# Five and six sevens in the first feed-forward's second product, with x loaded behind them

## The chip, the cores and the metric

The kernel runs on one core of one Trainium2 chip. The metric is the device time of one execution in microseconds; of several runs the median counts. Engines are named as in the profile: PE (TensorE: matmuls and transposes), DVE (VectorE), ACT (ScalarE), POOL (GpSimd, here almost only the issue of DMAs) and SP (SyncE, which issues the loads of weights).

## What is computed

One layer of a Conformer-like block over 256 tokens of width 2048, all in float32. Only the two feed-forwards are touched by the change; a mixer (convolution and gated spatial mixing) and a cross-attention with four heads stand between them.

```python
def swiglu_ffn(h, w_in, w_out):          # w_in 2048 x 11264, w_out 5632 x 2048
    gate, up = jnp.split(h @ w_in, 2, axis=-1)
    return (jax.nn.silu(gate) * up) @ w_out

x = x + 0.5 * swiglu_ffn(rms(x), ffn1_w_in, ffn1_w_out)
# ... mixer, cross-attention ...
x = x + 0.5 * swiglu_ffn(rms(x), ffn2_w_in, ffn2_w_out)
# final rms
```

## The kernel before

**A float32 product in three matmuls.** Every operand is kept as two parts of a reduced format, hi and lo, and a product is hi x hi + hi x lo + lo x hi. A weight tile ("raw", 128 x 1024, 512 KB) is loaded by SP; ACT casts it to hi (L396), DVE subtracts hi from raw to get lo (L397), both into a tile "hl". The transposed input (x_hl, or hA, hB, hC for the hidden values) has been split in the same way.

**Eights and sevens.** The k of a product are taken in pairs, two blocks of 128 rows of the weight. An "eight" multiplies a pair plainly: 24 matmuls of 512 columns, 12 for each of two weights. A "seven" takes the pair as a 2 x 2 block product with seven products instead of eight: 21 matmuls. Its weights are sums: DVE makes them with four half-width operations (L464, L465, L471, L478), and three and a half weights are cast and subtracted. Its left sides are sums too, prepared once (`out_sides`: one copy and two casts by ACT, four small sums and two subtracts by DVE for each pair that is ever a seven) and kept in `out_forms`. A weight of an eight feeds 12 matmuls in a row; of a seven's first weights PE uses two matmuls, then the next weight is wanted.

**The first feed-forward's second product** runs in two blocks of 1024 output columns (`out_block`, NG + 0 and NG + 1), each over 22 pairs in the order OUT_STEPS; OUT_S names the pairs that are sevens. In block 0 the transposes of the last hidden values ("turns", which write hB and hC, L131 and L132) run beside the first eights, so the sevens come behind them. In block 1 the sevens come first, with two eights between one and the next; the transposes of block 0's output o and the joins into x (`joins`, a DVE operation into xT, then x_hl and squares) run beside the eights that follow. When a block's last seven is done, its sums are copied to o and added there (ACT L515, DVE L516 to L519).

**Buffers.** Weights rotate through three tiles hl and a ring; in these blocks the ring has two tiles of more_out, whose other half holds four forms. Raw tiles rotate through four of a pool and those in `ff.raws`: for block 0 four raws_out, which lie in the place of xT (x is not needed there), and two raw_out; between the blocks xT is taken back and loaded again by two DMAs of POOL's queue (2 MB, L773), and block 1 has the pool and raw_out. When block 1's last seven is issued, the ring is emptied.

**Summed weights.** For some k (SUMMED) the lo part is not subtracted by DVE: ACT writes -raw and hi (L425, L426, in `summed`), and a DMA of POOL's queue adds the weight a second time from memory onto it (L427). The tile is hl_s; in the second feed-forward (`pair`) there is a second one up to group 7, and from group 8 on only one. The first two are issued in `run`: `summed(0)` in group 0 behind k = 13, `summed(1)` behind group 0.

**Order.** Instructions are placed on each engine by a scheduler that simulates the program with costs of its own, within the order of the code, the buffers and `tc.issue_after`. Each engine then runs its own list strictly in order: an instruction that waits holds all behind it.

## Time and profile before

| | us |
|---|---|
| runs | 2098.36, 2094.91, 2098.84; median 2098.36 |
| profiled execution | 2097.01 |
| its span in the trace | 2095.2 |
| PE busy | 2080.0 (99%) |
| DVE busy | 1621.0 (77%) |
| ACT busy | 1175.0 (56%) |

Busy shares are averages over stages; what counts for the time is where PE stands still. In a timeline the first number is the start and the second the length in us; matmuls are pipelined and their lengths overlap, so pace is read from start to start. In brackets stands how long the engine was idle before, and what it waited for.

### The profile page before, as it was taken

The page shows a single profiled execution, that of the slowest core. Times are in us where ns is not written, and L with a number is a line of the kernel's source. Part 1 is how long each engine was busy: PE and PEld are TensorE (multiplying, and loading weights), DVE is VectorE, ACT ScalarE, POOL GpSimd, SP SyncE. Part 2 cuts the span into 40 slices and gives each one's busy share as a digit, 9 for nine tenths or more (in the row PEclk, how much of TensorE's full clock was granted, in tenths as well). Part 3 has the DMA queues.
Part 4 walks back from the last instruction along what each step waited for, and adds up shares of the span by engine and source line. Part 5 has one row for each costly group of instructions (what it writes and reads, how often), then busy time and mean ns, then how long its engine had stood idle before and what let it go on. Part 6 is the DMA issues. An engine that isn't in the chain of part 4 may idle for free.

```text
span 2095.2 us, 26732 instructions
## 1 busy us (share of the span) xinstructions
PE 2080.0 (99%) x9765; PEld 1738.5 (83%) x9765; DVE 1621.0 (77%) x2300; ACT 1175.0 (56%) x1472; POOL 67.7 (3%) x83
## 2 busy tenths in 40 slices
PE   9999999999999999999999999999999999999998
PEld 8888888888788888888888898888888888888886
DVE  7888887877777679989877666778888878787754
ACT  8665666555546554445664455556665656554443
POOL 0000000000000000000000000000000000000000
PEclk9999999999999999999999999999999999999999
DMA  9787778755457566555555544677777777556664
GB/s 366 242 260 249 227 226 263 229 182 202 169 201 233 181 237 203 183 180 185 181 195 191 186 157 130 215 269 221 233 242 245 225 221 235 176 163 203 195 193 152
DMA packets 122532, 442.35 MB, mean 211 GB/s; under 512 B 13600, under 2 KB 13984, under 8 KB 122016
## 3 DMA queue, kind: packets, MB, share of 16 engines
q1 hardware_dynamic: 113184, 407.08, 56.4%
q0 software_dynamic: 8640, 32.51, 8.3%
q8 instruction: 76, 1.25, 0.2%
q10 hardware_dynamic: 576, 1.06, 0.1%
q14 instruction: 56, 0.46, 0.1%
HBM read 438.49 MB, written 2.10 MB: 210 GB/s over the span
## 4 chain that ended last, share of the span: by engine, by line
PE 81%; issue 15%; DMA 2%; POOL 1%; ACT 1%; DVE 1%; SPq 0%; DVEq 0%; POOLq 0%; ACTq 0%
PE acc L331 9%; PE acc L333 9%; PE acc L330 9%; PE acc L204 8%; PE acc L203 8%; PE acc L202 8%; PE acc L153 8%; PE acc L161 4%; PE acc L318 2%; PE acc L319 2%; PE acc L317 2%; PE aux L305 1%; POOL hl_s L427 1%; PE acc L1278 1%; PE acc L1277 1%
## 5 line engine op out<-in xcount | busy, mean ns | idle before, releaser
L123 ACT CAST hl<-raw 128x1024 fp32r<-128x1024 f32 (+1 forms) x315 | 327.1, 1040 | 356.1 <-PE acc L204 194.7
L124 DVE TENSOR_TENSOR hl<-raw,hl 128x1024 fp32r<-128x1024 f32 (+1 forms) x315 | 381.2, 1212 | 166.8 <-ACT hl L123 165.4
L397 DVE TENSOR_TENSOR hl<-raw,hl 128x1024 fp32r<-128x1024 f32 (+1 forms) x144 | 164.6, 1145 | 51.2 <-ACT hl L396 49.9
L396 ACT CAST hl<-raw 128x1024 fp32r<-128x1024 f32 (+1 forms) x144 | 141.0, 988 | 110.2 <-PE acc L333 51.4
L397 DVE TENSOR_TENSOR hl<-spare,hl 128x1024 fp32r<-128x1024 f32 (+1 forms) x128 | 146.9, 1152 | 37.3 <-ACT hl L396 34.6
L396 ACT CAST hl<-spare 128x1024 fp32r<-128x1024 f32 (+1 forms) x128 | 126.2, 993 | 73.3 <-PE acc L333 25.4
L331 PE MATMUL acc<-hl,x_hl 128*128 128x512 f32 x408 | 148.2, 391 | 0.1
L330 PE MATMUL acc<-hl,x_hl 128*128 128x512 f32 x408 | 142.4, 391 | 0.0
L333 PE MATMUL acc<-hl,x_hl 128*128 128x512 f32 x408 | 126.6, 389 | 0.0
L396 ACT CAST ring<-spare 128x1024 fp32r<-128x1024 f32 (+1 forms) x81 | 80.5, 998 | 59.3 <-issue 20.4
L397 DVE TENSOR_TENSOR ring<-spare,ring 128x1024 fp32r<-128x1024 f32 (+1 forms) x81 | 93.3, 1157 | 14.8 <-ACT ring L396 13.6
L203 PE MATMUL acc<-hl,x_hl 128*128 128x512 f32 x256 | 100.6, 393 | 0.0
L203 PE MATMUL acc<-hl,m_hl 128*128 128x512 f32 x256 | 100.3, 392 | 0.0
L204 PE MATMUL acc<-hl,m_hl 128*128 128x512 f32 x256 | 100.2, 392 | 0.0
L204 PE MATMUL acc<-hl,x_hl 128*128 128x512 f32 x256 | 99.9, 390 | 0.0
L331 PE MATMUL acc<-ring,x_hl 128*128 128x512 f32 x248 | 91.4, 389 | 0.0
L202 PE MATMUL acc<-hl,m_hl 128*128 128x512 f32 x256 | 90.9, 392 | 0.0
L202 PE MATMUL acc<-hl,x_hl 128*128 128x512 f32 x256 | 90.2, 392 | 0.0
L330 PEld LDWEIGHTS acc<-hl,x_hl 128*128 128x128 f32 x408 | 76.6, 188 | 16.2 <-ACT hl L396 0.4
L333 PEld LDWEIGHTS acc<-hl,x_hl 128*128 128x128 f32 x408 | 76.7, 188 | 16.0
L331 PEld LDWEIGHTS acc<-hl,x_hl 128*128 128x128 f32 x408 | 76.3, 188 | 16.4 <-DVE hl L397 0.8
L330 PE MATMUL acc<-ring,x_hl 128*128 128x512 f32 x248 | 88.8, 389 | 0.0
(515 smaller groups left out, 5115.2 us busy)
## 6 DMA issues: line engine op xcount, KB each, us to landing
spare<-in_ffn_w_in SPq DMA_DIRECT2D x185, 512.0 KB, 6.8
raw<-in_ffn_w_in SPq DMA_DIRECT2D x156, 512.0 KB, 6.3
raw<-in_ffn_w_out SPq DMA_DIRECT2D x135, 512.0 KB, 4.0
hl_s<-in_ffn_w_in POOLq DMA_DIRECT2D x44, 512.0 KB, 8.7
raw<-in_w_mix_vg SPq DMA_DIRECT2D x32, 512.0 KB, 4.5
raw<-in_w_k SPq DMA_DIRECT2D x32, 512.0 KB, 3.6
raw<-in_w_v SPq DMA_DIRECT2D x32, 512.0 KB, 4.3
raw<-in_w_mix_out SPq DMA_DIRECT2D x32, 512.0 KB, 4.6
```

The costliest lines, as they stand in the source:

```text
L123: nc.scalar.copy(out=hl[:, 0, :size], in_=raw[:, :size])
L124: newest[0] = nc.vector.tensor_tensor(out=hl[:, 1, :size], in0=raw[:, :size], in1=hl[:, 0, :size].bitcast(F32), op=ALU.subtract)
L153: done = nc.tensor.matmul(acc, lhsT=hi[:, k], rhs=xs[k], start=first and k == 0, stop=last and k == kk - 1, skip_group_check=True,)
L161: done = nc.tensor.matmul(acc[:, 0], lhsT=lo[:, k], rhs=xs[k][:, 0], start=False, stop=last and k == kk - 1, skip_group_check=True,)
L202: nc.tensor.matmul(acc[t], lhsT=x[:, 0, s], rhs=hi[:, k], start=k0 + k == 0, stop=False)
L203: nc.tensor.matmul(acc[t], lhsT=x[:, 0, s], rhs=lo[:, k], start=False, stop=False)
L204: nc.tensor.matmul(acc[t], lhsT=x[:, 1, s], rhs=hi[:, k], start=False, stop=k0 + k == nk - 1)
L330: nc.tensor.matmul(acc[t][g], lhsT=x[:, 0, s], rhs=hi[:, cols[g]], start=(t, g) in first, stop=False)
L331: nc.tensor.matmul(acc[t][g], lhsT=x[:, 0, s], rhs=lo[:, cols[g]], start=False, stop=False)
L333: nc.tensor.matmul(acc[t][g], lhsT=x[:, 1, s], rhs=hi[:, cols[g]], start=False, stop=last)
L396: self.cast = nc.scalar.copy(out=hl[:, 0, :n], in_=raw[:, :n])
L397: newest[0] = nc.vector.tensor_tensor(out=hl[:, 1, :n], in0=raw[:, :n], in1=hl[:, 0, :n].bitcast(F32), op=ALU.subtract)
```

## The change

Five things are changed. Sevens: three become five in block 0 and four become six in block 1, each followed by one eight while they last. Buffers: six forms instead of four, so the ring has one tile of more_out and a tile of its own, hl_out, which stays when the sevens end; the two raw_out are gone, and raws_out serve both blocks. x: its two loads are issued when block 1's last seven is, and the turns of block 0's output are handed out from step 14 on instead of step 10. Summed weights: the second feed-forward's groups 8 to 10 have k = 2 and 10 instead of 2, 7 and 13. `summed_then`: the first two summed weights are issued only behind the newest load and the newest cast. Line numbers of the kernel after are one higher around L396 (L397, L398), and more further down.

```diff
@@ -37,13 +37,14 @@
 PATTERNS = ("SCSCSCCC", "SCSCSCCC")
 
 SUMMED = ((2, 7, 13), (2, 7, 13))
-
-
-
-OUT_S = ((9, 12, 15), (9, 12, 15, 18))
+ALONE = (2, 10)
+
+
+
+OUT_S = ((9, 11, 13, 15, 17), (9, 11, 13, 15, 17, 19))
 OUT_STEPS = (
-    [0, 1, 2, 3, 4, 5, 6, 7, 8, 10, 11, 9, 13, 14, 12, 16, 17, 15, 18, 19, 20, 21],
-    [9, 0, 1, 12, 2, 3, 15, 4, 5, 18, 6, 7, 8, 10, 11, 13, 14, 16, 17, 19, 20, 21],
+    [0, 1, 2, 3, 4, 5, 6, 7, 8, 10, 9, 12, 11, 14, 13, 16, 15, 18, 17, 19, 20, 21],
+    [9, 0, 11, 1, 13, 2, 15, 3, 17, 4, 19, 5, 6, 7, 8, 10, 12, 14, 16, 18, 20, 21],
 )
 
 
@@ -404,7 +405,7 @@
             self.raw_at += 1
             raw = wraw.tile([P, 1024], F32, name="raw") if i < 4 else self.raws[i - 4]
 
-            nc.sync.dma_start(out=raw, in_=self.w_in[j, :, k] if j < NG else self.w_out[j - NG, :, k])
+            self.load = nc.sync.dma_start(out=raw, in_=self.w_in[j, :, k] if j < NG else self.w_out[j - NG, :, k])
             return raw
 
         def buffer(self, at):
@@ -425,6 +426,11 @@
             nc.scalar.activation(out=hl[:, 1], in_=raw, func=AF.Copy, scale=-1.0)
             nc.scalar.copy(out=hl[:, 0], in_=raw)
             nc.gpsimd.dma_start(out=hl[:, 1], in_=self.w_in[j, :, k], accum_op=ALU.add)
+
+        def summed_then(self, at):
+
+            with tc.issue_after(self.load.ins), tc.issue_after(self.cast.ins):
+                self.summed(at)
 
         def sides(self, i):
 
@@ -605,6 +611,9 @@
             acc = token_accs()
             sums = self.pattern_sums
             self.sums_at = [(j, k) for j in range(1, NG) for k in sums if j < NG - 1 or k < min(14, sums[-1])]
+            if self.pair:
+
+                self.sums_at = [at for at in self.sums_at if at[0] < 8] + [(j, k) for j in range(8, NG) for k in ALONE]
             for k in range(KD):
                 if k == 0 and early:
                     w = self.early(before)
@@ -617,12 +626,12 @@
                 if k == 13:
                     r = root()
                     nc.scalar.activation(out=st.tile([P, 1], F32, name="warm"), in_=ones[:, 0:1], func=AF.Silu)
-                    self.summed(0)
+                    self.summed_then(0)
             self.give(0, [acc[t][0] for t in range(2)], [acc[t][1] for t in range(2)], r)
             if more is not None:
                 more()
             if len(self.hls) > 1:
-                self.summed(1)
+                self.summed_then(1)
             turns = [self.turn(i) for i in range(2 * NG)]
             for j in range(1, NG):
                 if j < NG - 1:
@@ -747,10 +756,10 @@
         def turns_first(i):
             if i == 0:
                 more = big.tile([P, 4, 2, 1024], F32R, name="more_out", tag="S2")
-                ff.ring += [more[:, q] for q in range(2)]
-                forms = more[:, 2:].rearrange("p a two n -> p (a two n)")
+                ff.ring.append(more[:, 0])
+                forms = more[:, 1:].rearrange("p a two n -> p (a two n)")
                 ff.out_forms = [
-                    forms[:, q * 1024:(q + 1) * 1024].rearrange("p (f two n) -> p f two n", two=2, n=P) for q in range(4)
+                    forms[:, q * 1024:(q + 1) * 1024].rearrange("p (f two n) -> p f two n", two=2, n=P) for q in range(6)
                 ]
             next_turn()
             if i == 8:
@@ -758,7 +767,7 @@
                 ff.high.close()
                 pool = rest["pool"] = stack.enter_context(tc.tile_pool(name="ffn1", bufs=1, reuse_waits="tile"))
                 ff.sums = pool.tile([P, 1024], F32, name="sums_out")
-                ff.raws += [pool.tile([P, 1024], F32, name=f"raw_out{q}") for q in range(2)]
+                ff.ring.append(pool.tile([P, 2, 1024], F32R, name="hl_out"))
 
         def result():
             return rest["pool"].tile([P, 2, 2 * G], F32, name="o", bufs=2)
@@ -767,19 +776,20 @@
             return [turning(o, 2 * i * P, joins(8 * n + 2 * i)) for i in range(4)]
 
         o = ff.out_block(0, result, turns_first, next_turn)
-        ff.raws = ff.raws[4:]
-        xT = xt.tile([P, KD, T], F32, name="xT", tag="x")
-        for k in range(0, KD, 8):
-            nc.gpsimd.dma_start(out=xT[:, k:k + 8], in_=a["xT"][:, k:k + 8])
         turns += turned(o, 0)
 
         def beside_second(i):
+            nonlocal xT
             if i == OUT_STEPS[1].index(OUT_S[1][-1]):
-                ff.ring = []
+
+                ff.raws, ff.ring = [], ff.ring[1:]
+                xT = xt.tile([P, KD, T], F32, name="xT", tag="x")
+                for k in range(0, KD, 8):
+                    nc.gpsimd.dma_start(out=xT[:, k:k + 8], in_=a["xT"][:, k:k + 8])
                 rest["x_hl"] = gained_tile("S2")
-            elif i > 9:
+            elif i > 10:
                 beside(1.4)
-                if i % 2 == 0 and turns:
+                if i > 12 and i % 2 == 0 and turns:
                     turns.pop(0)()
 
         o = ff.out_block(1, result, beside_second)

```

How this moves instructions is shown at three places. First ACT, at the turn into block 0's sevens. Names: hC is the last part of the hidden values, tu and tg are a form's sums, sq is a copy beside them, more_out and hl_out are ring tiles, raw and raw_out are loaded weights, and sums_out are the sums of a seven. Before:

```order
L131 CAST more_out_3525<-tg_3876 128x2x128
L131 CAST hC_3867<-aux_3904 128x2x256
L131 CAST hC_3867<-aux_3927 128x2x256
L131 CAST hC_3867<-aux_3949 128x2x256
L396 CAST more_out_3525<-raw_out0_3961 128x1024
L396 CAST more_out_3525<-sums_out_3960 128x1024
L396 CAST hl_4044<-raw_out1_3962 128x1024
L396 CAST hl_4053<-raw_4031 128x1024
L396 CAST more_out_3525<-raw_4069 128x1024
```

After:

```order
L132 CAST hC_3893<-aux_3918 128x2x256
L132 CAST hC_3893<-aux_3953 128x2x256
L584 COPY sq_3927<-aux_3918 128x256
L132 CAST more_out_3525<-tu_3925 128x2x128
L132 CAST hC_3893<-aux_3976 128x2x256
L397 CAST hl_out_3988<-raw_4026 128x1024
L132 CAST more_out_3525<-tg_3926 128x2x128
L397 CAST hl_4030<-sums_out_3987 128x1024
L397 CAST more_out_3525<-raws_out_3478 128x1024
L397 CAST hl_4057<-raw_4026 128x512
```

Before, the casts of the three last turns stand alone ahead of the first weight (L396), which is an eight's; after, the casts of a form (tu, tg) stand between and behind them, and the first weight is a seven's.

Second PE, behind block 1's last seven. acc are output sums, aux here the transposes of block 0's output o. Before, the first of them come one eight behind that seven (hl_4797 is its second weight):

```order
L331 MATMUL acc_4421<-hl_4797,hA_3455 128x512
L333 MATMUL acc_4420<-hl_4797,hA_3455 128x512
L333 MATMUL acc_4421<-hl_4797,hA_3455 128x512
L305 MATMUL aux_4824<-ident_81,o_4274 128x128 x4
L330 MATMUL acc_4418<-hl_4840,hA_3455 128x512
L331 MATMUL acc_4418<-hl_4840,hA_3455 128x512
```

After:

```order
L320 MATMUL acc_4456<-more_out_3525,hC_3893 128x512
L319 MATMUL acc_4457<-more_out_3525 128x512
L320 MATMUL acc_4457<-more_out_3525 128x512
L306 MATMUL aux_5050<-ident_81,o_4345 128x128 x4
L318 MATMUL acc_4458<-hl_out_3988,hC_3893 128x512
L306 MATMUL aux_5131<-ident_81,o_4345 128x128 x4
L319 MATMUL acc_4458<-hl_out_3988,hC_3893 128x512
L320 MATMUL acc_4458<-hl_out_3988,hC_3893 128x512
L331 MATMUL acc_4456<-hl_out_3988,hA_3455 128x512
```

The transposes of the first two turns have moved into the last seven (L318 to L320 are its matmuls), between matmuls that wait for its last weight.

Third ACT, in the attention's last product (w_o). o_hl is the attention's output, hl_s2 and h8 are the second feed-forward's second summed weight and the tile it is loaded to. Before:

```order
L131 CAST o_hl_9168<-acc_10435 128x256
L123 CAST hl_10508<-raw_10506 128x512
L425 ACTIVATE hl_s2_11172<-h8_11173 128x1024
L426 CAST hl_s2_11172<-h8_11173 128x1024
L123 CAST hl_10528<-raw_10526 128x1024
L123 CAST hl_10557<-raw_10555 128x1024
L280 ACTIVATE x_hl_10466<-xT_4411,pv_82 128x256
```

After:

```order
L132 CAST o_hl_9220<-acc_10487 128x256
L124 CAST hl_10560<-raw_10558 128x512
L124 CAST hl_10580<-raw_10578 128x1024
L124 CAST hl_10609<-raw_10607 128x1024
L281 ACTIVATE x_hl_10518<-xT_4858,pv_82 128x256
L254 ACTIVATE ss_10519<-xT_4858 128x256
```

The two operations on the summed weight are gone from between the casts of w_o's weights; they stand in the second feed-forward's group 0.

## Rows read from the trace of the kernel before

**Rows 1.** The page, part 1: busy us (share of span) xinstructions

```profile
PE 2080.0 (99%) x9765; PEld 1738.5 (83%) x9765; DVE 1621.0 (77%) x2300; ACT 1175.0 (56%) x1472; POOL 67.7 (3%) x83
```

**Rows 2.** Waits of PE, by releaser: us in total, times, longest

```profile
PE acc L331 <- DMA hl_s<-in_ffn_w_in: 1.9, 3, 0.8
```

**Rows 3.** Windows: us, busy (x count) by engine, PEclk, DMA share, GB/s

```profile
540.00:560.00 20.00, 19.45 (x86) 15.74 (x85) 17.92 (x21) 10.85 (x13) 0.00 (x0) 1.00 0.61 205
600.00:620.00 20.00, 20.00 (x90) 16.56 (x89) 17.20 (x20) 10.64 (x12) 0.00 (x0) 1.00 0.72 233
```

**Rows 4.** Timeline of DVE, then ACT, in block 0: start, length, instruction

```profile
552.88 1.22 DVE L397 TENSOR_TENSOR more_out<-raws_out,more_out 128x1024 fp32r<-128x1024 f32 x1
554.02 0.69 DVE L471 TENSOR_TENSOR raw<-sums_out,raw 128x512 f32<-128x512 f32 x1
554.62 0.68 DVE L478 TENSOR_TENSOR raws_out<-raws_out 128x512 f32<-128x512 f32 x1
...
546.80 1.05 ACT L396 CAST hl<-raws_out 128x1024 fp32r<-128x1024 f32 x1
547.75 1.05 ACT L396 CAST hl<-sums_out 128x1024 fp32r<-128x1024 f32 x1
```

**Rows 5.** Timeline of PE, then ACT, before block 0's sevens

```profile
531.99 0.39 PE L330 MATMUL acc<-hl,hB 128*128 128x512 f32 x1
...
533.53 1.20 PE L330 MATMUL acc<-more_out,hB 128*128 128x512 f32 x4 [0.45 <-ACT more_out L396]
...
542.92 0.40 PE L330 MATMUL acc<-more_out,hB 128*128 128x512 f32 x1
531.95 0.59 ACT L131 CAST hC<-aux 128x512 fp32r<-128x512 f32 x1 [3.76 <-PE aux L305]
532.43 1.05 ACT L396 CAST more_out<-raw_out 128x1024 fp32r<-128x1024 f32 x1
```

**Rows 6.** Lines by form, 500 to 530 us: a form's cast

```profile
L131 ACT CAST more_out<-tu 128x256 fp32r<-128x256 f32 x3 | 1.2, 400 | 0.7 <-DVE tu L582 0.7
```

**Rows 7.** Timeline of ACT, then PE, in the w_o product

```profile
1301.87 1.06 ACT L425 ACTIVATE hl_s<-h 128x1024 fp32r<-128x1024 f32 x1 [2.03 <-DMA h<-in_ffn_w_in]
1302.84 1.03 ACT L426 CAST hl_s<-h 128x1024 fp32r<-128x1024 f32 x1
1304.86 1.43 PE L153 MATMUL acc<-o_hl,hl 128*128 128x512 f32 x5 [1.94 <-ACT hl L123]
```

**Rows 8.** Timeline of ACT, then PE, in the first feed-forward's group 0

```profile
32.72 1.04 ACT L425 ACTIVATE hl_s<-spare 128x1024 fp32r<-128x1024 f32 x1
...
35.87 0.61 PE L333 MATMUL acc<-hl,x_hl 128*128 128x512 f32 x2
...
37.76 0.50 PE L331 MATMUL acc<-hl,x_hl 128*128 128x512 f32 x1
```

**Rows 9.** Timeline of PE at two of the three waits for hl_s

```profile
1754.16 0.39 PE L318 MATMUL acc<-hl,x_hl 128*128 128x512 f32 x1
...
1755.52 0.39 PE L330 MATMUL acc<-hl_s,x_hl 128*128 128x512 f32 x1
1756.52 0.72 PE L331 MATMUL acc<-hl_s,x_hl 128*128 128x512 f32 x2 [0.60 <-DMA hl_s<-in_ffn_w_in]
...
1797.92 0.39 PE L330 MATMUL acc<-hl_s,x_hl 128*128 128x512 f32 x1
1799.06 0.73 PE L331 MATMUL acc<-hl_s,x_hl 128*128 128x512 f32 x2 [0.75 <-DMA hl_s<-in_ffn_w_in]
```

**Rows 10.** Transfers into xT, issue to landing

```profile
DMA to landing us min/median/max: 5.2/6.7/8.2
```

**Rows 11.** Windows in the hole of the w_o product and after the last matmul

```profile
1302.00:1305.00 3.00, 1.06 (x7) 0.78 (x7) 1.50 (x5) 3.00 (x4) 0.89 (x1) 1.00 0.45 153
2087.00:2089.00 2.00, 0.00 (x0) 0.00 (x0) 1.06 (x4) 1.54 (x4) 0.67 (x1) 0.99 0.63 260
2089.00:2091.00 2.00, 0.00 (x0) 0.00 (x0) 1.60 (x5) 0.92 (x2) 0.59 (x1) 0.50 0.78 314
```


## The prediction

> **What bounds the kernel now.** I read the page's busy times first: TensorE is busy for 2080.0 of 2095.2 us, VectorE for 77%, ScalarE for 56% [rows 1]. So time is won by taking matmuls away, or by closing one of the few holes in PE; work given to another engine costs only where PE then waits. The waits of PE come second. Of them the change touches one that is listed under one line: three waits for hl_s, 1.9 us in all [rows 2]. Third come the windows around the two out blocks. Where PE is full, VectorE is busy 17.20 of 20 us (86%), and still PE shows no wait; the one window that is not full is the turn into block 0's sevens [rows 3]. So the question is what four more sevens do there, where VectorE has least to give.
>
> The pace is needed for everything that follows. A full subtract takes VectorE 1.14 us from start to start (552.88 to 554.02), a half-width operation 0.60, a full cast takes ScalarE 0.95 (546.80 to 547.75) [rows 4].
>
> **The change part by part.**
>
> *Four eights become sevens.* 24 matmuls become 21, four times: 12 fewer. A matmul of 512 columns starts 0.227 us after the one before it (six of them from 1754.16 to 1755.52) [rows 9]: 12 x 0.227 = -2.7 us, all on the path, since PE is full.
>
> What it adds on VectorE: a seven has three full subtracts, one half-width and four half-width sums, 3 x 1.14 + 5 x 0.60 = 6.4 us, against its 21 x 0.227 = 4.8 us of PE; an eight has two subtracts, 2.3 us against 5.4. Before, a seven stands with two eights: 11.0 us of VectorE for 15.7 of PE, 70%. After, sevens and eights alternate: 8.7 for 10.2, 85%. That is the density of the full window of [rows 3], which runs without a wait, so steady running should cost nothing; what costs is each place where VectorE or ScalarE begins without a lead, because only 1.5 us of lead is made up in 10.2.
>
> *The turn into block 0's sevens.* Before, from 531.99 to 542.92 PE starts 35 matmuls (L330 at 531.99 and those up to 542.92); 35 x 0.227 = 7.9, so 3.0 us of these 10.9 are lost: ScalarE casts the last hC at 531.95, then the first weight at 532.43, and PE has that weight at 533.53 [rows 5]. The first weight feeds an eight, so PE then has 12 matmuls, 2.7 us, in which the next casts run. After, two turns stand together and the first weight's cast stands behind two casts of hC, a copy and one cast of a form instead of behind one cast of hC: 0.59 [rows 5] and 0.40 [rows 6] more, 1.0 us. And it feeds a seven, of which a weight serves two matmuls before the next is wanted: 0.95 of cast against 0.45 of PE, 0.5 us for each of three more weights, 1.5 us. Together +2.5 us; bounds +1.5 (the form's cast hidden) and +4.0 (VectorE's subtracts, 1.14 each, late as well).
>
> *The rest of block 0.* No row shows alternating sevens behind an empty lead. By the 85% it is 0; by one reuse of a ring slot that is cast again as soon as PE lets it go, one cast and half a subtract, some 1.5. I take +1.0.
>
> *Block 1's six sevens.* Below: 0, by the same window. Above: the first seven starts behind block 0's four adds into o (4 x 0.60) with no lead, three weights at 0.5 = 1.5 us; and at the end the four adds of block 1's o, two subtracts of the eights behind it and the adds of the memory's squares stand in VectorE's order ahead of the last half-width subtract of the last seven, for which PE waits: 2.4 + 2.3 + about 1, with the transposes of block 0's o, which were moved to just there and wait for VectorE too: 6 to 7. So 0 to +8. I take +3.0, since the nearest row is the turn into block 0's sevens before, where a lead lost once costs 3.0 [rows 5].
>
> *xT behind the sevens.* Before, it came between the blocks, from POOL's queue. Now the transfer can start only when the last seven's raw tiles are free. Behind it stand, in order, VectorE's join of the first transposes (and then every later subtract) and ScalarE's x_hl operations (and then the next weight's cast), and PE waits for those weights. The two transfers took 5.2 and 8.2 us from issue to landing [rows 10]; the first join needs the first. PE has some 49 matmuls of work that is cast before that wait, 11.1 us, against 5.2 + 0.6 for the join + 1.9 for ScalarE's x_hl (no row shows them there; two casts' time) + 0.95 + 1.14: 9.8. Cost 0, bounds 0 and +3 (if the first lands with the second).
>
> The Trainium skill ("DMA: Bandwidth & Descriptors", section "Anatomy of one DMA — SWDGE (gpsimd) path") gives a transfer from this queue 2.0 us plus its bytes at 436 GB/s: 4.4 us for the first 1 MB, an estimate from that page. The trace's 5.2 is later and decides; by the page the cover would be 0.8 us longer, and the sum the same.
>
> *The w_o product of the attention.* ScalarE waits 2.03 us there for the load of the second feed-forward's summed weight, spends two operations on it from 1301.87, and only then casts the weight for which PE sits idle for 1.94 us [rows 7]. The change issues these operations behind the newest load and cast of the second feed-forward: they leave this place. What is next is the cast itself, whose load was issued before the one that ScalarE waited for. -1.9 us; bound -1 if the second weight there lands late.
>
> *The first feed-forward's start.* The same move takes L425 and L426 (32.72) from ahead of three casts. From 35.87 to 37.76 PE starts six matmuls, 1.36 us of 1.89 [rows 8]: -0.5 us.
>
> *Summed weights of the second feed-forward's last groups.* With one buffer, only 45 matmuls, 10 us, lie between k = 13 of one group and k = 2 of the next, and PE waits for the addition: 1755.52 to 1756.52 and 1797.92 to 1799.06 hold one matmul each, 0.77 + 0.91 us, and the slow pair behind each about 0.1 more [rows 9]: 1.9 us for these two. With k = 2 and 10 there are 78 to 88 matmuls between, 18 to 20 us. The third, into group 8, comes from a group that keeps its 13 and stays. Two summed weights fewer give VectorE two subtracts, which PE does not wait for there. -1.9 us.
>
> **Sum:** -2.7 - 1.9 - 0.5 - 1.9 = -7.0; +2.5 + 1.0 + 3.0 + 0 = +6.5; together -0.5. The profiled execution took 2097.01 us (span 2095.2), so 2096.5; the median of the runs lies 1.35 above that execution, so I say **2097**.
>
> **The rivals.**
>
> *A, the lead holds.* Density of 85% costs nothing, as in [rows 3], in both blocks; only the turn costs: -7.0 + 2.5 = -4.5, 2092.5. For it: 20 us at 86% with a full PE. Against: that window is an average of subtracts for eights, which PE takes 12 matmuls at a time.
>
> *B, VectorE ends last at the end of block 1's sevens.* The adds into o and the joins stand ahead of the subtract for which PE waits; it decides from the point at which VectorE reaches the last seven with less than its 6 us of adds and subtracts in hand. -7.0 + 2.5 + 1.5 + 8 = +5.0, 2102; with xT 3 late as well, 2105: slower, against the median.
>
> *C, the change doesn't do what it says at hl_s.* The waits move to k = 10: -1.9 is lost, 2098.5. Some 18 us from one to the next, where now 10 us lack one, speak against it.
>
> *D, TensorE's clock falls in the longer hole.* It is 1.00 across the hole of w_o, 0.99 in the second after the last matmul and 0.50, 1.2 GHz, from 2089 on, with no matmul in that window or in the one before it [rows 11]. The new hole, some 2.6 us at its longest, lies between. If it fell, the 21 matmuls of the seven behind it would take 4.8 us more: 2101.5. The Trainium skill ("TensorE: Matmul & The Clock Gate", Part 1) says that "the default state is throttled, and activity releases the throttle"; the last row agrees, and no hole inside the kernel shows it.
>
> **How the numbers follow.** Forecast 0.42, A 0.33, B 0.19, C 0.04, D 0.02. A run of this kernel can be told from no change by about 0.2%, 4.2 us around 2098.36. Faster by more is A, 0.33; within it are the forecast, C and D, 0.48; slower by more is B, 0.19, whose lower time lies at the bound. The range runs from A with the turn at its lower bound and a little of the holes' spread (2091) to between B's two times (2104).
>
> **What would show it.** In the profile after: no wait of PE in w_o and none at 36 to 38 us; one wait for hl_s of three; a hole of some 2.5 us at the turn into block 0's sevens, and matmuls missing from the following 20 us against 90 of a full window; in block 1, waits of PE for VectorE at the last seven (rival B if 5 us or more, A if none); ScalarE's first x_hl behind xT not followed by a wait of PE. The forecast is wrong if the two blocks together lose less than 5 us or more than 11 (before: 3.0).

## The result: slower, and where the time went

The kernel after takes 2103.51 us (median of 7 runs, 2102.72 to 2104.46) against 2095.77 of the kernel before (7 runs): a ratio of 1.0032, 95% interval 1.0021 to 1.0044. The forecast was 2097 us, no change that a run could tell. The spans of the two profiled executions differ by 7.5 us (2102.7 and 2095.2).

The page of the kernel after, part 1, in the form of [rows 1]:

```profile
PE 2082.3 (99%) x9753; PEld 1738.2 (83%) x9753; DVE 1639.9 (78%) x2338; ACT 1179.5 (56%) x1484; POOL 66.0 (3%) x81
```

PE has fewer instructions and yet more busy time, in part because some of its matmuls ran at half clock (PEclk in the windows below). PE's waits after (engine line <- released by: us in total, times, longest), where before one line of hl_s stood beside one of w_o; a wait of 1.1 us at the program's start, which both kernels have, is left out:

```profile
PE acc L318 <- ACT hl_out L397: 3.8, 3, 1.8
PE acc L331 <- ACT hl_out L397: 1.4, 1, 1.4
PE acc L319 <- DVE more_out L398: 1.3, 2, 1.1
PE acc L318 <- ACT more_out L397: 1.3, 2, 1.0
PE aux L306 <- DVE o L524: 0.8, 1, 0.8
PE acc L332 <- DMA hl_s<-in_ffn_w_in: 0.4, 1, 0.4
```

The first five of these are all in the out blocks, and two of them name one tile, hl_out. Windows of the kernel after (us, busy of PE, PEld, DVE, ACT and POOL with their counts, PEclk, DMA share, GB/s), to be read beside [rows 3]:

```profile
530.00:536.00 6.00, 4.05 (x11) 2.37 (x11) 6.00 (x11) 4.02 (x6) 0.00 (x0) 0.72 0.01 3
600.00:620.00 20.00, 19.75 (x87) 15.78 (x86) 18.40 (x21) 10.21 (x12) 0.00 (x0) 1.00 0.64 215
652.00:656.00 4.00, 1.92 (x8) 0.98 (x7) 2.94 (x4) 2.87 (x5) 0.00 (x0) 1.00 0.14 37
656.00:660.00 4.00, 1.95 (x9) 1.13 (x8) 3.55 (x7) 1.57 (x2) 0.00 (x0) 1.00 0.93 334
660.00:664.00 4.00, 2.06 (x8) 1.32 (x9) 3.82 (x6) 3.12 (x5) 1.10 (x2) 0.72 0.73 209
664.00:668.00 4.00, 4.00 (x11) 3.14 (x10) 2.65 (x6) 0.59 (x2) 0.00 (x0) 0.50 0.99 408
1300.00:1310.00 10.00, 10.00 (x65) 9.07 (x65) 5.40 (x10) 4.85 (x10) 0.00 (x0) 1.00 0.45 143
```

PE is half empty from 652 to 664, the end of block 1's sevens, and runs at half clock behind that; the hole of w_o ([rows 7]) is closed. The kernel before is full at that place:

```profile
640.00:660.00 20.00, 20.00 (x92) 16.55 (x91) 15.44 (x22) 11.67 (x20) 0.00 (x0) 1.00 0.64 210
```

A sum by place is possible for all of PE's matmuls: the time from one start to the next, less the pace of its kind (0.227 us for 512 columns, 0.120 for 256, 0.109 for a transpose). It is worked out from all rows of both traces:

| place | lost before, us | lost after, us |
|---|---|---|
| first feed-forward, start | 0.65 | 0 |
| turn into block 0's sevens (520 to 550) | 3.0 | 6.15 |
| block 1, start of the sevens (610 to 630) | 0 | 1.85 |
| block 1, last seven (650 to 670) | 0 | 10.1 |
| mixer, at 770 | 0 | 0.65 |
| w_o | 2.2 | 0 |
| hl_s, groups 8 to 10 | 2.75 | 0.65 |
| all other places, about half of it at the program's start | 5.7 | 5.1 |
| all of PE | 14.3 | 24.5 |

24.5 - 14.3 = 10.2, less 12 x 0.227 = 2.7 for the matmuls taken away, is 7.5: the difference of the spans. Of the 15.75 us that are lost anew, 10.1, about two thirds, are at one place. Without them the spans would differ by 2.6 us the other way.

**The last seven of block 1.** PE's timeline there (start, length; in brackets the idle time before, and its releaser):

```profile
652.61 0.39 PE L320 MATMUL acc<-hl,hC 128*128 128x512 f32 x1
654.02 0.50 PE L318 MATMUL acc<-more_out,hC 128*128 128x512 f32 x1 [1.03 <-ACT more_out L397]
...
655.81 0.50 PE L319 MATMUL acc<-more_out,hC 128*128 128x512 f32 x1 [1.06 <-DVE more_out L398]
...
659.21 0.50 PE L318 MATMUL acc<-hl_out,hC 128*128 128x512 f32 x1 [1.76 <-ACT hl_out L397]
660.55 0.66 PE L306 MATMUL aux<-ident,o 128*128 128x128 f32 x4 [0.84 <-DVE o L524]
...
661.49 0.42 PE L320 MATMUL acc<-hl_out,hC 128*128 128x512 f32 x1
663.30 2.08 PE L331 MATMUL acc<-hl_out,hA 128*128 128x512 f32 x4 [1.40 <-ACT hl_out L397]
```

and ScalarE's:

```profile
651.05 0.42 ACT L254 ACTIVATE sm<-raw 128x256 f32<-128x256 f32 x1 [5.54 <-DMA raw<-in_memT]
651.38 0.71 ACT L257 ACTIVATE sq<-raw 128x256 f32<-128x256 f32 x2
651.99 1.04 ACT L397 CAST hl<-raw 128x1024 fp32r<-128x1024 f32 x1
652.93 1.03 ACT L397 CAST more_out<-raws_out 128x1024 fp32r<-128x1024 f32 x1
...
657.59 1.04 ACT L397 CAST hl<-raw 128x1024 fp32r<-128x1024 f32 x1 [2.46 <-DMA raw<-in_ffn_w_out]
658.54 0.62 ACT L397 CAST hl_out<-raws_out 128x512 fp32r<-128x512 f32 x1
660.19 1.05 ACT L397 CAST hl<-raw 128x1024 fp32r<-128x1024 f32 x1 [1.03 <-DMA raw<-in_ffn_w_out]
...
662.22 1.03 ACT L397 CAST hl_out<-raw 128x1024 fp32r<-128x1024 f32 x1
```

Three things are to be seen. ScalarE stands for 5.54 us for a load of the memory, with the last seven's casts behind it in its list; later it stands again, 2.46 us for the load of a weight, with the half-weight's cast behind it. PE stands five times, and nothing of the eights that follow runs in between, although two of their weights are cast into tiles hl at 657.59 and 660.19: in PE's list they come behind the eight in hl_out, at 668.58. And the last seven's half-weight (658.54) and the next eight's first weight (662.22) are cast into the same tile, hl_out: the second cast can come only when PE is through with the first (661.49), and PE waits for it again at 663.30. In this trace ScalarE also works on the memory just before that cast (L257, 661.59 to 662.3), so it alone does not tell which held it; the first run below does. The first of the three is the one that strikes the eye. The experiments show that it is the third, with the order of PE's list that goes with it.

### The profile page after: what moved, and what is told of

It reads as the page before. It is cut to its first block, busy times and chain, and to the rows that moved or that the text cites. A ratio compares the mean times of both kernels' runs of the same rounds, so it can differ in the third digit from the quotient of the medians.

```text
span 2102.7 us, 26743 instructions
## 1 busy us (share of the span) xinstructions
PE 2082.3 (99%) x9753; PEld 1738.2 (83%) x9753; DVE 1639.9 (78%) x2338; ACT 1179.5 (56%) x1484; POOL 66.0 (3%) x81
## 4 chain that ended last, share of the span: by engine, by line
PE 83%; issue 12%; DVE 2%; DMA 1%; ACT 1%; POOL 1%; DVEq 0%; POOLq 0%; ACTq 0%
PE acc L331 10%; PE acc L332 10%; PE acc L334 10%; PE acc L154 8%; PE acc L204 8%; PE acc L205 8%; PE acc L203 8%; PE acc L162 4%; PE acc L319 3%; PE acc L320 3%; PE acc L318 3%; PE aux L306 1%; PE aux L319 1%; PE aux L320 1%; PE aux L318 1%
## 5 line engine op out<-in xcount | busy, mean ns | idle before, releaser
L124 ACT CAST hl<-raw 128x1024 fp32r<-128x1024 f32 (+1 forms) x315 | 327.1, 1041 | 352.4 <-PE acc L205 190.0
L125 DVE TENSOR_TENSOR hl<-raw,hl 128x1024 fp32r<-128x1024 f32 (+1 forms) x315 | 381.2, 1212 | 162.3 <-ACT hl L124 161.0
L398 DVE TENSOR_TENSOR hl<-raw,hl 128x1024 fp32r<-128x1024 f32 (+1 forms) x152 | 174.0, 1149 | 57.4 <-ACT hl L397 56.0
L397 ACT CAST hl<-raw 128x1024 fp32r<-128x1024 f32 (+1 forms) x152 | 149.1, 992 | 114.4 <-PE acc L334 46.7
L398 DVE TENSOR_TENSOR hl<-spare,hl 128x1024 fp32r<-128x1024 f32 (+1 forms) x125 | 144.7, 1162 | 30.6 <-ACT hl L397 28.1
L397 ACT CAST hl<-spare 128x1024 fp32r<-128x1024 f32 (+1 forms) x125 | 124.4, 1002 | 66.3 <-PE acc L334 28.3
L332 PE MATMUL acc<-hl,x_hl 128*128 128x512 f32 x388 | 140.8, 390 | 0.0
L331 PE MATMUL acc<-hl,x_hl 128*128 128x512 f32 x388 | 135.8, 391 | 0.0
L334 PE MATMUL acc<-hl,x_hl 128*128 128x512 f32 x388 | 120.5, 389 | 0.0
L397 ACT CAST ring<-spare 128x1024 fp32r<-128x1024 f32 (+1 forms) x83 | 82.1, 993 | 60.8 <-PE acc L334 20.1
L398 DVE TENSOR_TENSOR ring<-spare,ring 128x1024 fp32r<-128x1024 f32 (+1 forms) x83 | 95.2, 1151 | 21.1 <-ACT ring L397 20.6
L332 PE MATMUL acc<-ring,x_hl 128*128 128x512 f32 x276 | 101.2, 389 | 0.0
L204 PE MATMUL acc<-hl,x_hl 128*128 128x512 f32 x256 | 100.7, 393 | 0.3 <-DVE hl L125 0.3
L205 PE MATMUL acc<-hl,x_hl 128*128 128x512 f32 x256 | 100.0, 391 | 0.0
L331 PE MATMUL acc<-ring,x_hl 128*128 128x512 f32 x276 | 98.5, 389 | 0.0
L203 PE MATMUL acc<-hl,x_hl 128*128 128x512 f32 x256 | 90.9, 392 | 0.0
L334 PE MATMUL acc<-ring,x_hl 128*128 128x512 f32 x276 | 86.1, 389 | 0.0
L334 PEld LDWEIGHTS acc<-hl,x_hl 128*128 128x128 f32 x388 | 72.9, 188 | 15.2
L331 PEld LDWEIGHTS acc<-hl,x_hl 128*128 128x128 f32 x388 | 72.9, 188 | 15.1
```

The costliest lines, as they stand in the source:

```text
L124: nc.scalar.copy(out=hl[:, 0, :size], in_=raw[:, :size])
L125: newest[0] = nc.vector.tensor_tensor(out=hl[:, 1, :size], in0=raw[:, :size], in1=hl[:, 0, :size].bitcast(F32), op=ALU.subtract)
L203: nc.tensor.matmul(acc[t], lhsT=x[:, 0, s], rhs=hi[:, k], start=k0 + k == 0, stop=False)
L204: nc.tensor.matmul(acc[t], lhsT=x[:, 0, s], rhs=lo[:, k], start=False, stop=False)
L205: nc.tensor.matmul(acc[t], lhsT=x[:, 1, s], rhs=hi[:, k], start=False, stop=k0 + k == nk - 1)
L331: nc.tensor.matmul(acc[t][g], lhsT=x[:, 0, s], rhs=hi[:, cols[g]], start=(t, g) in first, stop=False)
```

## The experiments

Each diff is against the kernel after unless the text says otherwise. Times are medians; the kernel before ran beside all of them (2095.2 to 2095.8). The kernel after was not run beside them, so differences to its 2103.51 are good to about that spread, 0.7 us.

**The squares of the memory later.**

```diff
             elif i > 10:
-                beside(1.4)
+                if i > 13:
+                    with tc.issue_after(ff.load.ins), tc.issue_after(ff.cast.ins):
+                        beside(1.4)
```

> The kernel after, with the squares of the memory (load of memT, four ScalarE operations, four VectorE adds each) begun three steps later in block 1 and queued behind the newest weight's load and cast. Theory: the 10 us lost at the end of block 1's sevens begin with ScalarE's wait of 5.5 us for memT ahead of two casts, while VectorE idles as long; without it the two holes at 652.8 to 655.8 are gone, what stays at the last seven is 3 us at most, TensorE's clock stays at 1.00 there, and the time falls by 7 us to about 2096.5. Rival: VectorE's adds into o, the moved transposes and the half-width subtract set the end by themselves; then holes of 6 us or more stay, and the time is 2100 or more.

Measured: 2103.16 us. ScalarE's wait of 5.5 us for the load is gone, and with it most of the first two holes; 8.6 us of 10.1 are still lost. The later waits stay as they were (PE):

```profile
657.80 0.50 PE L318 MATMUL acc<-hl_out,hC 128*128 128x512 f32 x1 [1.67 <-ACT hl_out L397]
659.13 0.66 PE L306 MATMUL aux<-ident,o 128*128 128x128 f32 x4 [0.83 <-DVE o L524]
...
662.09 2.08 PE L331 MATMUL acc<-hl_out,hA 128*128 128x512 f32 x4 [1.14 <-ACT hl_out L397]
```

And with nothing else ahead of it, the second cast into hl_out waits for PE's last matmul of the first (ScalarE):

```profile
660.99 1.04 ACT L397 CAST hl_out<-raw 128x1024 fp32r<-128x1024 f32 x1 [3.25 <-PE acc L320]
```

The theory falls: the longest wait in the trace was not what the end hung on.

**One more eight ahead of block 0's first seven.**

```diff
-    [0, 1, 2, 3, 4, 5, 6, 7, 8, 10, 9, 12, 11, 14, 13, 16, 15, 18, 17, 19, 20, 21],
+    [0, 1, 2, 3, 4, 5, 6, 7, 8, 10, 12, 9, 14, 11, 16, 13, 18, 15, 19, 17, 20, 21],
```

> The kernel after, with one more eight ahead of the first seven in block 0 (12 ahead of 9, and so on). Theory: the 6.1 us lost from 526 to 541 come from the first weight's cast behind the last turns and from sevens that want a weight for every two matmuls; behind an eight the hole is under 2 us, the clock stays at 1.00, at most 3 us are lost in all and the time is about 2100.5. Rival: the lead is lost to the turns themselves, whatever follows; then 5 us or more are lost there again and the time is 2103 or so.

Measured: 2106.73 us, 3 us slower than the kernel after, as the rival had it. 6.1 us are lost at the turn again, and 2.4 from 560 to 580, where the kernel after loses nothing. The turn's loss now stands behind this wait of ScalarE for a ring tile:

```profile
534.29 1.04 ACT L397 CAST more_out<-raw 128x1024 fp32r<-128x1024 f32 x1 [3.39 <-PE acc L334]
```

L334 is a matmul of the weight that lay in more_out just before: again one tile twice in a row. This row, and the 662.22 above, led to the next theory.

**The summed weights' part alone.** The kernel before with ALONE and `summed_then`:

```diff
+ALONE = (2, 10)
...
+            if self.pair:
+                self.sums_at = [at for at in self.sums_at if at[0] < 8] + [(j, k) for j in range(8, NG) for k in ALONE]
...
-                    self.summed(0)
+                    self.summed_then(0)
...
-                self.summed(1)
+                self.summed_then(1)
```

> The kernel before with the summed weights' part of the change alone (k = 2 and 10 from group 8 on, the first two issued behind the newest load and cast); both out blocks as before. Theory: it gains what the trace after shows outside the out blocks, 2.1 at hl_s, 2.2 in w_o, 0.6 at the first feed-forward's start: 4.9 us, about 2091. Rival: the gain is taken back in the second feed-forward's first groups, where the two operations now stand: 2094 or more.

Measured: 2092.69 us, ratio to before 0.9987 (0.9978 to 0.9996), -2.6 us in the comparison and -4.8 us by the spans (2090.4 against 2095.2, one execution each). That lies between theory and rival. The gain is real and holds by itself; of the 4.8 us the medians bear out little more than half.

**Squares later and one more eight.** The first two diffs together.

> The kernel after with both edits, squares later and one more eight ahead of block 0's first seven. Theory: the two losses are apart, 7 and 3 us come back, about 2093.5, faster than the kernel before. Rival: a lead that is not lost at one place is lost at the next, and it stays at 2098 or more.

Measured: 2104.26 us: the rival. 8.1 us are lost at the last seven and 4.4 at the turn, and 2.9 us turn up in block 0 from 560 to 580, where the kernel after loses nothing. Neither edit touched the cause.

**The whole switch four steps later.**

```diff
-            if i == OUT_STEPS[1].index(OUT_S[1][-1]):
+            if i == 14:
...
-            elif i > 10:
+            elif i > 14:
                 beside(1.4)
-                if i > 12 and i % 2 == 0 and turns:
+                if i in (16, 18, 19, 20) and turns:
```

> The kernel after, with everything that ends the sevens' phase in block 1 four steps later: the raw tiles in x's place and both ring tiles stay until step 14, and x, the squares of the memory and the turns of block 0's output come behind that. Taking the squares away alone gave back 1.5 us of 10 at the last seven, so the theory now: what ends last there is the switch itself at the last seven (fewer raw tiles and one ring slot less while the last seven still needs them, and the moved transposes, for whose PSUM VectorE must first read the sevens' sums). Then here 2 us at most are lost from 640 to 680, and the time is 2095.5. Rival: VectorE's density of six sevens; then 6 us or more are lost at the last seven as before and the time is 2100 or more.

Measured: 2098.31 us, -5.2 against the kernel after. Nothing is lost from 640 to 680, so six dense sevens with their adds into o cost nothing there, and the rival of VectorE's density falls. But 3.9 us are lost in the mixer from 720 to 780, where the kernel after loses 1.0; PE waits there mostly for VectorE's subtracts (1.5 us in three waits). That they are late because x comes later is likely and was not tried apart.

**The rotation moved on by one slot.** The weight tiles rotate by a counter modulo the number of tiles, three and those of the ring. When the ring falls from two to one, the modulus falls from five to four, and the counter, which stood behind the fifth tile, points to the fourth: hl_out again.

```diff
                 ff.raws, ff.ring = [], ff.ring[1:]
+                ff.at += 1
```

> The kernel after, with the rotation of the weight tiles moved on by one slot when the ring shrinks at block 1's last seven, and nothing else. As it is, the last half-weight of the last seven and the next eight's first weight are both cast into hl_out, one right behind the other. Theory (one slot used twice in a row): the cast for the eight no longer waits for PE, eights stand ready while the last seven waits for VectorE, and 6 us or more of the 10 come back: 2097.5 or less. Rival (raw tiles, squares and transposes): 2 us at most come back, 2101.5.

Measured: 2096.61 us, -6.9, level with the kernel before (ratio 1.0003, 0.9993 to 1.0012). 1.5 us are lost at the last seven (650 to 670), and 0.9 up to 680. ScalarE waits for the memory's load as before; the window of PE around it, and the one behind:

```profile
651.06 0.42 ACT L254 ACTIVATE sm<-raw 128x256 f32<-128x256 f32 x1 [5.55 <-DMA raw<-in_memT]
...
652.00:656.00 4.00, 3.44 (x13) 2.00 (x12) 2.93 (x3) 3.41 (x5) 0.00 (x0) 1.00 0.17 27
656.00:660.00 4.00, 4.00 (x20) 3.26 (x20) 4.00 (x7) 1.88 (x3) 0.00 (x0) 1.00 0.83 250
```

The same wait of 5.55 us costs almost nothing, because PE has something else to do: the next eights, whose weights no longer need the tile of the last seven, run between the last seven's matmuls. Behind the transposes, PE's list shows it (hl_4910 is an eight's weight, hl_out the last seven's half-weight):

```order
L306 MATMUL aux_5050<-ident_81,o_4345 128x128 x4
L331 MATMUL acc_4456<-hl_4910,hA_3455 128x512
L331 MATMUL acc_4457<-hl_4910,hA_3455 128x512
L331 MATMUL acc_4459<-hl_4910,hA_3455 128x512
L318 MATMUL acc_4458<-hl_out_3988,hC_3893 128x512
```

The last seven itself ends no sooner. First VectorE's subtract of its half-weight in the kernel after and here, then the last of its matmuls here, which in the kernel after stands at 661.49:

```profile
660.41 0.69 DVE L398 TENSOR_TENSOR hl_out<-raws_out,hl_out 128x512 fp32r<-128x512 f32 x1
```

```profile
660.42 0.69 DVE L398 TENSOR_TENSOR hl_out<-raws_out,hl_out 128x512 fp32r<-128x512 f32 x1
662.66 0.39 PE L320 MATMUL acc<-hl_out,hC 128*128 128x512 f32 x1
```

So what ScalarE and VectorE wait for around the last seven was not shortened; PE had work beside it. One line moved both the tile and the order that follows from it; the runs do not part the two.

**The transposes of block 0's output later.** `newest_mm` holds the last matmul of an eight:

```diff
                 if i > 12 and i % 2 == 0 and turns:
-                    turns.pop(0)()
+                    with tc.issue_after(newest_mm[0].ins):
+                        turns.pop(0)()
```

> The kernel after, with the transposes of block 0's output queued on PE behind the newest matmul of the eight beside which the program has them, instead of inside the last seven. Theory (the transposes wait there for PSUM that VectorE has still to read, with the last seven's matmuls behind them): the waits of PE in front of the transposes go, 2 to 3 us come back, about 2101. Rival (the slot): the last seven waits as long for its half-weight, 2103.

Measured: 2105.68 us, the rival or worse. PE no longer waits for VectorE ahead of the transposes, but 10.9 us are lost there, as the waits for hl_out are longer (2.3, 1.1 and 1.1 us). So the moved transposes are not the cause: they stood in a hole that was there.

**The rotation moved on already in block 0**, when hl_out joins the ring:

```diff
                 ff.ring.append(pool.tile([P, 2, 1024], F32R, name="hl_out"))
+                ff.at += 1
```

> The kernel after, with the rotation of the weight tiles moved on by one slot when hl_out joins the ring ahead of block 0's sevens, so that the first seven's first weight is cast into a tile hl instead of hl_out. hl_out lies where the last hidden values were, and its cast stands behind the last turns' casts; in hl it stands ahead of the last three. Theory: the hole ahead of the first seven falls from 2 us to under 1, the clock stays at 1.00 from 530 to 536, and 2 to 3 us of the 6 come back: about 2101. Rival (sevens want a weight for every two matmuls, wherever the first one lies): the hole moves by two matmuls and the time stays at 2103.

Measured: 2094.34 us, -9.2 against the kernel after; level with before (0.9995, 0.9985 to 1.0004). More than expected, and elsewhere: the turn into block 0's sevens still loses 5.0 us (6.15 after), but nothing is lost at 610 to 630 or at the last seven. The counter stays one slot on, and the last half-weight is cast into a tile hl (at 648.02) instead of hl_out; why 610 to 630 is clean was not tried apart. Some 2.8 us come up new between 660 and 680. At the turn the rival is nearer: the first weight is there, and PE waits 2.3 us for the second.

**Pair 18 instead of 19 as the sixth seven**, on top of the last; 18 and 19 also change places in block 1's order:

```diff
-OUT_S = ((9, 11, 13, 15, 17), (9, 11, 13, 15, 17, 19))
+OUT_S = ((9, 11, 13, 15, 17), (9, 11, 13, 15, 17, 18))
```

> The kernel with the rotation moved on by one slot (e9_first: 2094.3), and pair 18 instead of pair 19 as the sixth seven of block 1. The form of pair 19 is made from the last turn but two, so its seven operations (a copy, four sums, two casts with their subtracts) stand between the last turns and the first seven's sums; that of pair 18 is made one turn earlier. Theory: what is left of the turn's loss (5 us in e9_first against 3.0 in the kernel before) is this chain on ScalarE and VectorE: the hole of 2.3 us falls by 1 us or more, the clock stays nearer to 1.00, and the time falls by 1 to 3 us to about 2092.5. Rival: the hole is set by the transposes and hC alone, and the time stays at 2094.

Measured: 2094.06 us, which the runs cannot tell from 2094.34. In the trace the turn loses 4.0 us instead of 5.0, the clock stays at 1.00, and 0.7 us more are lost from 660 to 680. The chain is worth 1 us there, in one execution; in the time it is open.

**Work in the hole of the turn**, the kernel after with ten matmuls that count for nothing; `newest_t` holds the last transpose:

```diff
+            if j == NG and "5" not in self.begun:
+                with tc.issue_after(newest_t[0].ins):
+                    for _ in range(10):
+                        nc.tensor.matmul(
+                            b["5"], lhsT=form[0][0], rhs=self.hA[:, 0].rearrange("p a t -> p (a t)"), start=True, stop=True
+                        )
```

> The kernel after, with ten added matmuls of 512 columns behind the last turn's transposes, into the sums' bank that the first seven clears when it starts: 2.3 us of work in the hole of 2 us ahead of the first seven, with no effect on what follows. Theory (half of what is lost there behind the hole is the clock, 0.50 from 532 to 535): the clock stays at 1.00, the first matmuls of the seven start 0.23 us apart instead of 0.43, and in spite of ten more matmuls the time is the same or 1 us lower, 2102.5 to 2103.5. Rival (the clock plays no part, the casts set the pace): the same pace of the first seven with the clock at 1.00, and 0.5 us or more longer.

Measured: 2104.50 us, 1 us more than the kernel after (unclear beside its range). The clock stays at 1.00. From the last transposes to the first eight's weight behind the first seven, first the kernel after, then this one (PE):

```profile
529.39 0.66 PE L306 MATMUL aux<-ident,h 128*128 128x128 f32 x4 [0.40 <-DVE hC L133]
...
538.99 0.96 PE L331 MATMUL acc<-hl,hB 128*128 128x512 f32 x3 [0.45 <-ACT hl L397]
```

```profile
528.96 0.66 PE L307 MATMUL aux<-ident,h 128*128 128x128 f32 x4 [0.40 <-DVE hC L134]
...
538.56 0.96 PE L332 MATMUL acc<-hl,hB 128*128 128x512 f32 x3 [0.45 <-ACT hl L398]
```

9.60 us in both, in one execution each. So casts and subtracts set the pace of the first seven; a slower PE only fills time in which it would have waited. The rival holds: at this place the clock costs nothing that these runs show.

**No wait for hl_s at all**, on top of pair 18:

```diff
-                self.sums_at = [at for at in self.sums_at if at[0] < 8] + ...
+                self.sums_at = [at for at in self.sums_at if at[0] < 8 and at != (7, 13)] + ...
```

> As e10_form, and k = 13 of group 7 in the second feed-forward is no longer summed, so that no wait for hl_s of the three is left. Theory: the wait of 1 to 2 us at 1712 goes, 1.5 us against e10_form. Rival: the added subtract is late there instead, no change.

Measured: 2091.93 us, ratio to before 0.9984 (0.9975 to 0.9994). The third wait is gone and 2.1 us with it: faster than both kernels.

**The same without the new sevens**: the kernel before with ALONE, `summed_then` and without group 7's k = 13.

> The kernel before with the summed weights' part of the change alone, and without the sum at k = 13 of group 7 (as e12_third has it); three and four sevens as before. It tells what the twelve matmuls are worth once the rotation is right (e12_third: 2091.9). Theory: nothing, since 2.7 us of matmuls stand against 1 us more lost at the turn and 3 us where x is loaded while weights are wanted: 2091 to 2092. Rival: the sevens still pay, and this one is slower than e12_third, 2093.5.

Measured: 2091.15 us, ratio 0.9979 (0.9970 to 0.9988), the fastest of all, if only by 0.8 us in another comparison. By the traces e12_third, with 12 matmuls fewer (2.7 us), loses 4.0 us at the turn and 2.9 from 660 to 680; here 3.0 and none. What is lost from 660 to 680 begins, in e12_third, with a load of a weight that lands late while x's two megabytes are on their way too and the DMA engines are busy for 0.98 of the time (ScalarE; then the window):

```profile
658.54 1.05 ACT L397 CAST hl_out<-raw 128x1024 fp32r<-128x1024 f32 x1 [5.92 <-DMA raw<-in_ffn_w_out]
...
650.00:660.00 10.00, 10.00 (x48) 8.27 (x47) 5.87 (x10) 2.42 (x3) 0.00 (x0) 1.00 0.98 383
```

Behind that cast stand, each in order, VectorE's join into xT, ScalarE's x_hl, and at 663.91 the cast for which PE then waits 1.4 us. That x's transfer is what holds the load was not tried apart. So even with the rotation put right, no gain of twelve matmuls fewer can be told: the intervals of the two ratios overlap.

## Why the prediction was wrong

- *The forecast as a whole.* 2103.51 lies inside the stated range, 2091 to 2104, but only by way of rival B, whose mechanism did not hold: luck. By the forecast's own sign it was wrong: the two blocks lose 18.1 us, not 5 to 11. Its base was off as well. The median of 2098.36 came from three runs; over seven it is 2095.77, below the profiled execution and not 1.35 above it. And 2096.5 with 1.35 added is 2097.9, not 2097.
- *Four eights become sevens, -2.7.* Right: PE's count fell by 12 and the sum by place closes with it.
- *The turn into block 0's sevens, +2.5.* Right in place, mechanism and size: +3.1 (6.15 against 3.0), PE waiting 1.7 us for the first weight and 0.2 to 0.5 us for those behind it; e11_fill shows that the casts and subtracts set the pace there. The added hole was expected to leave the clock alone, and did not.
- *Rest of block 0, +1.0.* Nothing was lost there.
- *Block 1, +3.0 of 0 to 8.* **This is the step that failed**: 12.0 us, 1.9 from 610 to 630 and 10.1 at the last seven, beyond the upper bound. The value was borrowed from a place where a lead is lost once, and the bounds were built from VectorE's work, on the premise that PE's only work there waits for it. What kept the eights from filling PE's waits was a tile, and 2.6 of the 10.1 us came on top from the half clock behind them (last section), for which the term had nothing. The order shown ahead of the prediction has it: in the second fence after, L320 reads hl_out for the last seven, and the next line, L331, reads hl_out for an eight. The text of the change has it too, `ff.ring[1:]` under a counter taken modulo the ring. The buffers were read there for how many there are, not for which one comes next. e6_slot shows it: one slot on gives back 6.9 us, with the last seven ending no sooner; e5_late shows that density costs nothing there. What the 1.9 at 610 to 630 come from stays open.
- *xT, 0.* In the kernel after no wait of PE stands behind it: landed 5.4 and 8.7 us after issue (5.2 and 8.2 in [rows 10]). That was under cover of the larger loss; with the rotation right up to 3 us come up at 660 to 680 (2.8 in e9_first, 2.9 in e12_third), the upper bound, on the path that the term names: join, x_hl, the next cast. That x's transfer sets it off is likely, not shown.
- *w_o, -1.9; first feed-forward, -0.5; hl_s, -1.9.* Right: -2.2, -0.65 and -2.1 in the traces.
- *Rivals.* B had place and sign (slower, at the end of block 1's sevens) with 0.19, but not its mechanism. Its own sign was 5 us or more of waits for VectorE at the last seven: they are 1.9 us, against 4.2 for ScalarE, and the same subtract at the same time costs little in e6_slot. D came true as an event, and its price of 4.8 us at the turn did not: e11_fill. The clock's fall that did cost, at the last seven, it did not see. C and A did not happen.
- *What was late next.* The gains of 7 us were argued from single holes and stood in the traces (by the medians, e3_summed bears out 2.6 of the 4.8 that are not matmuls); the losses were summed as if each stage's order were given. It is not: the tile that a cast is given decides which matmuls the scheduler can put beside it.

## What to carry to other kernels

Where buffers rotate by a counter modulo their number, a change of that number in the middle is a change of which buffer comes next: write out the tiles in order across the seam, and look for one that is used twice in a row. The longest wait in the trace need not be the one that costs: ask what PE could have run meanwhile, and why that was not ready. Where casts set the pace, as at the turn here, a stretch took the same 9.60 us whether PE ran at full or half clock, so there neither a fuller PE nor a higher clock mends it; where PE has its weights, half clock is paid for in full.

## What the hardware showed that was not expected

TensorE's granted clock fell inside the kernel, twice; in the kernel before, no hole had shown that. Ahead of block 0's sevens it is 1.00 (2.4 GHz) until 532 and 0.50 (1.2 GHz) from 532 to 535, after a stretch in which PE ran only four transposes and one matmul between 529 and 532 (idle 0.40 and 1.73 us). The second time it is 1.00 until 661 and 0.50 from 662 to 668, after PE was busy for 3.9 of the 8 us from 652 to 660. In the kernel before, in the hole of w_o, 1.94 us, it had stayed at 1.00 [rows 11]. Where PE was not waiting for casts the price is plain: the 12 matmuls from 663.30 take 5.28 us until the next weight at 668.58, against 12 x 0.227 = 2.7, so 2.6 of the 10.1 us lost at the last seven are the clock; where it was waiting for them, as at the turn, the price was nothing. One window of each level in the kernel after:

```profile
531.00:532.00 1.00, 0.23 (x1) 0.23 (x2) 1.00 (x3) 1.00 (x3) 0.00 (x0) 1.00 0.00 0
534.00:535.00 1.00, 1.00 (x3) 0.79 (x3) 1.00 (x3) 0.07 (x1) 0.00 (x0) 0.50 0.00 0
```
